# Moving nine adds of squares from VectorE to GpSimd, and a scaled copy ahead of a square, in a two-layer decoder step

## The chip, the core and the metric

The kernel runs on one core of a Trainium2 chip, in one launch. The metric is the device time of that launch in microseconds. Engines are named as in the profile: PE is TensorE, PEld its weight loads, DVE is VectorE, ACT is ScalarE, POOL is GpSimd and SP is SyncE, which issues most of the transfers.

## What is computed

One inference step of a two-layer decoder for 512 prompt tokens and 8 sample tokens (520 together), width 1024, all in 32-bit floats. Each layer is a half-weighted SwiGLU block, a token mixer, and a second SwiGLU block; the first layer mixes by causal window means, the second by window attention. A norm stands ahead of every one of them, and one at the end:

```
def _rmsnorm(x, g):
    xf = x.astype(jnp.float32)
    y = xf * lax.rsqrt(jnp.mean(xf * xf, axis=-1, keepdims=True) + EPS)
    return (y * g.astype(jnp.float32)).astype(x.dtype)

def _swiglu(x, wg, wu, wd):
    return (jax.nn.silu(x @ wg) * (x @ wu)) @ wd

# every layer l:
x = x + 0.5 * _swiglu(_rmsnorm(x, norm_g[l, 0]), ...)
h = _rmsnorm(x, norm_g[l, 1])
x = x + mixer(h)
x = x + 0.5 * _swiglu(_rmsnorm(x, norm_g[l, 2]), ...)
# at the end
y = _rmsnorm(x, final_norm_g)
```

The outputs are y of both groups, the last rows of the pooling input, and the windows of keys and values. The change touches only the sums of squares that the norms need.

## The kernel before

The residual stream lies transposed in SBUF: eight channel tiles x of 128 channels by 520 tokens. Weights stream from HBM as raw tiles; each is split into a rounded high part and a remainder (`wh` by ACT, `wl` by DVE, both 128x512), and every product is three matmuls: high by high, high by low, low by high. Activations are split likewise (`xh` and `xl`, `th` and `tl`, `hh` and `hl`). Part of the products are done by a seven-product scheme, which needs sums of weight blocks: S, summed by transfers on POOL's queue (L649, L372), and sums on DVE (L379, L386).

A norm is not applied ahead of a product. The products take x scaled by g alone, and the token's factor is put in behind them. So a norm runs beside the products: ACT squares each x tile into `sq` (two buffers), DVE adds the eight squares into `acc` (a copy for the first tile, seven adds), PE sums `acc` over the channels by matmuls with a vector of ones (L845, "column sums"), DVE works out the root in a chain of small instructions that ends in `r_tok` (L857 to L869), and PE turns `r_tok` round into a row for all partitions (L885, L886), which ACT copies into `R`.

Three places of this kind concern the change:

- *Behind the first half layer*, ahead of the pooling mixer, the function `delayed` squares tile k when it is finished (L1482) and adds the square when the next tile comes (L1459, L1461). The last tile's work is pinned to the written order. PE passes from the down projection to the mixer's first products (L1700) and then to the column sums.
- *At the start of the second half layer* (the first layer's second SwiGLU block), eight calls of `square` (L816, L818, L823) stand ahead of it.
- *In the tail*, `final_after` calls `square` and then `scaled` for each finished x tile; `scaled` (L2444) makes the copy `xg`, scaled by the final norm's g, that PE turns back into token rows (`turn`, L2424 and L2425).

What sets the order. In the first place and the tail, the tile framework's scheduler, but for what is pinned. In the second, a planner written in the kernel, the class `Queues`: every step is added with an engine ("A" for ACT, "V" for DVE, "P" for PE, "N" for others), a cost, a due time and the keys that it reads and writes; PE's products advance the planner's clock, and a step is issued into its engine's order when its predecessors are done by the planner's account. A step on "N" costs nothing there:

```
cost = 0 if eng == "N" else cols * self.unit if eng == "P" else 50 + 0.93 * cols if eng == "A" else 70 + 1.04 * cols
```

The engines then run their orders one after the other, with waits on one another where data need it.

Of the kernel before, what the change touches and what calls it, by code (L numbers as in the profile page):

```python
# [15 lines left out]
ALU = mybir.AluOpType  # L16
# [4 lines left out]
KT = 8  # L21
# [3 lines left out]
TOK = SP + NS  # L25
# [522 lines left out]
def yoco_step(ctx, tc, ins, outs):  # L548
    nc = tc.nc
# [3 lines left out]
    V, S, T = nc.vector, nc.scalar, nc.tensor  # L553
# [16 lines left out]
    Q = Queues(1344)  # L570
# [3 lines left out]
    def duo():  # L574

        cnt[0] += 1
        k = Q.key("ps", 4)
        Q.bank = (*k, 0), (*k, 1)
        return pools[0].tile([P, 2, 512], F32, tag="ps", name=f"ps{cnt[0]}")
# [9 lines left out]
    def pair(tags, shape, dtype=F32R):  # L589

        return tuple(big.tile(shape, dtype, tag=t, name=t) for t in tags)
# [6 lines left out]
    def by_slots(on, busy=0):  # L598

        W.pin = lambda ins: ins  # L600
        if on:
            pinned.enter_context(
                tc.manual_schedule(
                    engines={mybir.EngineType.PE, mybir.EngineType.DVE, mybir.EngineType.Activation}
                )
            )
            W.begin_slots(Q)
            Q.start(W.ng, busy)
            W.plan()
        else:  # L610
            Q.stop()
            W.q = None
            assert W.ns == W.nh and not Q.pending
            pinned.close()

    def seq(ins):

        return later(ins) if ordered[0] else ins
# [17 lines left out]
    def later(ins):  # L636

        return tc.keep_in_program_order(ins)


    W = Weights(nc, rawp, splp, 2, 5)
# [131 lines left out]
    acc = cp.tile([P, TW], F32, name="acc")  # L773
# [4 lines left out]
    def gcol(n, k):  # L778
        return gT[:, n * 8 + k : n * 8 + k + 1]
# [29 lines left out]

        return bank[:, :H].rearrange("p (a b) -> p b a", b=2)  # L810

    def square(k, pool, tag, order=lambda ins: ins):
        sq = pool.tile([P, TOK], F32, tag=tag, name="sq", bufs=1 if tag == "rp0" else 2)
        key = Q.key(tag, 2)
        G = (*key, 0), (*key, 1)
        Q.add("A", 520, lambda: order(S.activation(sq, x[k], AF.Square)), W.ng + 2, (), G)  # L816
        if k == 0:
            Q.add("V", 520, lambda: order(V.tensor_copy(acc[:, :TOK], sq)), W.ng + 2, G, (("acc",),))  # L818
        else:
            Q.add(  # L820
                "V",
                520,
                lambda: order(V.tensor_tensor(acc[:, :TOK], acc[:, :TOK], sq, op=ALU.add)),  # L823
                W.ng + 2,
                G,
                (("acc",),),
            )

    pss_ = [None]
    nu = [2]  # L830

# [606 lines left out]
    def ff_pool():  # L1438
        return tc.tile_pool(name="ff", bufs=2, reuse_waits="tile")

    def deferred(n, tmp, tag, tags, lst, w=TOK):

        def f(k):
            z = pair(tags, [P, w])
            split(tuple(a[:, :TOK] for a in z), x[k], gcol(n, k))
            lst.append(z)
            square(k, tmp, tag)

        return f

    def delayed(n, tmp, tag, tags, lst, w):

        made = {}

        def rest(k):
            z, sq = made.pop(k)
            pin = later if k + 1 >= PIN0 else seq
            if k == 0:
                pin(V.tensor_copy(acc[:, :TOK], sq))  # L1459
            else:  # L1460
                pin(V.tensor_tensor(acc[:, :TOK], acc[:, :TOK], sq, op=ALU.add))  # L1461
            if k < KT - 2:
                low(k, z, pin)
            else:
                lows.append((k, z))

        def low(k, z, pin):
            h, l = (a[:, :TOK] for a in z)
            pin(V.scalar_tensor_tensor(l, x[k], gcol(n, k), h.bitcast(F32), op0=ALU.mult, op1=ALU.subtract))

        lows = []

        def f(k):
            if k:
                rest(k - 1)
            z = pair(tags, [P, w])
            sq = tmp.tile([P, TOK], F32, tag=tag, name="sq")
            high = lambda: S.activation(z[0][:, :TOK], x[k], AF.Copy, scale=gcol(n, k))
            if k < KT - 1:
                high()  # L1480
            pin = later if k + 1 >= PIN0 else seq
            pin(S.activation(sq, x[k], AF.Square))  # L1482
            if k == KT - 1:
                high()
            lst.append(z)
            made[k] = z, sq
            if k == KT - 1:
                rest(k)
                for v in lows:
                    low(*v, later)  # L1490

        return f

    def start_hooks(tmp, n, tt, late, norm_tok=rstd_tok):

        steps = sums(tmp, n, tt, W.next_sum())
        step = lambda: next(steps, None)
        there[0] = False
        none = lambda: None

        norm0 = norm_tok

        def norm_all():
            rstd_all()
            known()

        kinds = {"-": none, "s": step, "n": norm0, "a": norm_all}

        def many(word):
            def f():  # L1510
                for c in word:
                    kinds[c]()

            return f

        return [many(w) for w in late.split()]
# [3 lines left out]
    with ff_pool() as tmp:  # L1520
# [69 lines left out]
        first = duo(), duo()  # L1590
# [13 lines left out]
        for k in range(KT):  # L1604
            if k > 1:
                quarter(k, 0)
            if k + 2 < KT:
                x_tile(k + 2)()
            quarter(k, 1)
            if k == 1:  # L1610
                ws += [W.get(), W.get()]
            if k > 2:
                W._split(k + 1)
            for i in {}.get(k, ()):
                square(i, tmp, "g", later)
        by_slots(True, 0)
        for k in range(0, KT):
            square(k, tmp, "g")
# [52 lines left out]
    with tc.tile_pool(name="pm", bufs=2, reuse_waits="tile") as pm:  # L1671
# [33 lines left out]
        def high(gi, tau):  # L1705
            r = r_tok[:, tau : tau + 1] if tau < 4 else r5
            later(S.activation(back(zs[gi][tau][0]), apart(places[gi][tau]), AF.Copy, scale=r))
# [103 lines left out]
    with ff_pool() as tmp:  # L1811


        later(nc.sync.dma_start(pool_sample[0, :, 0:14, :], state_pool[0, :, 1:15, :]))
        for dst, src in ((k_win_s, cache_k), (v_win_s, cache_v)):
            later(
                nc.sync.dma_start(
                    dst[:, 0:127].rearrange("b s g d -> b s (g d)"), src[:, 1:128].rearrange("b s g d -> b s (g d)")
                )
            )  # L1820
        later(nc.sync.dma_start(sraw, attn_sinks.broadcast_to([P, 16])))
        for b in range(NS):
            later(nc.sync.dma_start(sink_s[b * 16 : (b + 1) * 16, 0:1], attn_sinks.rearrange("l h -> h l")))
        by_slots(True, 2)
        for m in range(KT):
            square(m, tmp, "g")
        tt = {}
        ffn(1, tmp, mov2, start_hooks(tmp, 2, tt, "- - ns s a s s s s s s"), tt, HH, deferred(N_KV, tmp, "g", XX, movk))

# [153 lines left out]
    with tc.tile_pool(name="at", bufs=2, reuse_waits="tile") as at:  # L1983
# [61 lines left out]
        class Unit:  # L2045
# [71 lines left out]
            def turn(self, bi):  # L2117
                if bi == 0:
                    self.pts = {}
                    self.both = {}  # L2120
                b = self.bs[bi]
                self.both[bi] = single()
                for kt in (0,) if b == 0 else (0, 1):
                    for e in range(2):
                        z = self.sm[:, 2 * bi + e, 256 - self.keys(bi) + kt * P :][:, :P]
                        later(T.transpose(self.both[bi][:, kt * 256 + e * P : kt * 256 + (e + 1) * P], z, ident))  # L2126
# [48 lines left out]
        first = W.ng  # L2175
# [223 lines left out]
    with ff_pool() as tmp:  # L2399
# [41 lines left out]
        def scaled(k, c):  # L2441
            if k not in xgs:
                xgs[k] = tmp.tile([P, TOK], F32, tag=("t", "sa")[k % 2], name="xg")
            seq(S.activation(xgs[k][:, c], x[k][:, c], AF.Copy, scale=gcol(N_FIN, k)))  # L2444

        def final_after(k):
            square(k, tmp, "g")
            scaled(k, slice(0, TOK))
            if k == 1:
                later(S.activation(warm, ones[:, 0:1], AF.Sqrt))  # L2450
            waiting.append(k)
            W.ahead += 2
            if len(waiting) > 2:
                k = waiting.pop(0)
                turn(k)(*engines[k % 2])
# [45 lines left out]
        def tail(hs):  # L2501
# [118 lines left out]
            ordered[0] = False  # L2620

        ffn(3, tmp, mov6, start_hooks(tmp, 5, tt, "ss ns sss a ss s", norm_tok), tt, HH, final_after, by_parts=tail)


# [29 lines left out]
```

## Time and profile before

| What | Value |
|---|---|
| Time, median of 3 runs | 1519.8 us (1519.19 to 1526.01) |
| Profiled execution, its own time | 1520.76 us |
| Its span, first to last instruction | 1517.8 us |
| Mean granted PE clock | 0.998 |
| PE busy | 1503.1 us (99%) |
| DVE busy | 1385.1 us (91%) |
| ACT busy | 991.1 us (65%) |
| POOL busy | 308.0 us (20%) |

Times in the profile are in microseconds from the first instruction of that execution. A matmul's end is modelled, and matmuls overlap; a busy PE need not be one at its peak. Idle time of an engine stands in brackets in front of the instruction that ended it, with what released it. L and a number is a line of the kernel before.

### The profile page before, as it was taken

The numbers are of one execution on the slowest core, as the hardware profiler recorded it, in microseconds if no ns is written. First come the engines' busy times: TensorE is split into PE (matmuls) and PEld (weight loads), VectorE is DVE, ScalarE is ACT, GpSimd is POOL, SyncE is SP. The second block draws the span as 40 slices with busy tenths as digits, with TensorE's granted clock in tenths as the row PEclk, the third lists the DMA queues.
The fourth block names the chain that finished last, engine by engine and source line by source line (L and its number), as shares of the span: only waits on it lengthen the run. The fifth ranks groups of instructions, "written<-read, shape, count | busy, mean of one in ns | idle before, by whom it ended". The sixth has DMA issues, their size and how long they took to land.

```text
span 1517.8 us, 34874 instructions
## 1 busy us (share of the span) xinstructions
PE 1503.1 (99%) x13342; PEld 1489.3 (98%) x13342; DVE 1385.1 (91%) x2790; ACT 991.1 (65%) x2025; POOL 308.0 (20%) x346
## 2 busy tenths in 40 slices
PE   9999999999999999999999999999999999999997
PEld 8999999999999999999999999999999999999997
DVE  6999999979999999879999999876887899999977
ACT  6765665657675675656665675655886666666655
POOL 1122222000122222100322222101551122222200
PEclk9999999999999999999999999999999999999999
DMA  9589899763599999835898998854313589999941
GB/s 246 121 194 208 182 202 207 178 182 100 118 205 199 194 204 199 177 119 127 198 204 189 197 206 194 184 175 115 75 43 92 111 185 198 200 194 193 207 132 57
DMA packets 418834, 254.61 MB, mean 168 GB/s; under 512 B 13134, under 2 KB 399174, under 8 KB 418628
## 3 DMA queue, kind: packets, MB, share of 16 engines
q1 hardware_dynamic: 339822, 187.60, 44.7%
q0 software_dynamic: 75520, 60.00, 28.4%
q10 hardware_dynamic: 3326, 4.79, 1.0%
q8 instruction: 104, 1.70, 0.5%
q14 instruction: 62, 0.51, 0.1%
HBM read 218.07 MB, written 6.11 MB: 148 GB/s over the span
## 4 chain that ended last, share of the span: by engine, by line
PE 85%; DVE 8%; ACT 3%; DMA 2%; issue 1%; POOL 0%; DVEq 0%; ACTq 0%
PE ps L935 61%; PE ps L905 17%; DVE wl L476 2%; DMA pr<-in_bands_dram 1%; PE pv L2153 1%; ACT wh L472 1%; PE ps L2068 1%; PE pv L2126 1%; PE pv L1700 1%; PE pv L1749 1%; DMA S<-in_ffn_w_down_dram 0%; DVE acc L823 0%; PE ps L2521 0%; PE ps L2530 0%; PE pv L905 0%
## 5 line engine op out<-in xcount | busy, mean ns | idle before, releaser
L472 ACT ACTIVATE wh<-raw 128x512 fp32r<-128x512 f32 (+1 forms) x725 | 443.8, 624 | 181.1 <-PE ps L935 69.0
L476 DVE TENSOR_TENSOR wl<-raw,wh 128x512 fp32r<-128x512 f32 (+1 forms) x725 | 482.8, 681 | 21.1 <-ACT wh L472 19.5
L935 PE MATMUL ps<-th,wh 128*128 128x260 f32 x1216 | 334.5, 275 | 0.3 <-DVE sb L1241 0.3
L935 PE MATMUL ps<-tl,wh 128*128 128x260 f32 x1216 | 334.4, 275 | 0.0
L935 PE MATMUL ps<-th,wl 128*128 128x260 f32 x1216 | 334.4, 275 | 0.0
L935 PE MATMUL ps<-xh,wh 128*128 128x260 f32 x896 | 247.2, 276 | 0.3 <-ACT sb L1209 0.3
L935 PE MATMUL ps<-xl,wh 128*128 128x260 f32 x896 | 246.4, 275 | 0.0
L935 PE MATMUL ps<-xh,wl 128*128 128x260 f32 x896 | 246.4, 275 | 0.0
L935 PEld LDWEIGHTS ps<-th,wh 128*128 128x128 f32 x1216 | 231.0, 190 | 0.5 <-DVE sb L1241 0.5
L935 PEld LDWEIGHTS ps<-tl,wh 128*128 128x128 f32 x1216 | 231.0, 190 | 0.0
L935 PEld LDWEIGHTS ps<-th,wl 128*128 128x128 f32 x1216 | 231.0, 190 | 0.0
L935 PE MATMUL ps<-hh,wh 128*128 128x260 f32 x656 | 181.0, 276 | 0.1
L935 PE MATMUL ps<-hl,wh 128*128 128x260 f32 x656 | 180.6, 275 | 0.4 <-DVE hl L624 0.3
L935 PE MATMUL ps<-hh,wl 128*128 128x260 f32 x656 | 180.4, 275 | 0.0
L649 POOL DMA_DIRECT2D S<-in_ffn_w_up_dram x76 | 100.3, 1327 | 373.6 <-DMA S<-in_ffn_w_up_dram 122.3
L935 PEld LDWEIGHTS ps<-xh,wh 128*128 128x128 f32 x896 | 170.2, 190 | 1.5 <-ACT sb L1209 0.8
L935 PEld LDWEIGHTS ps<-xh,wl 128*128 128x128 f32 x896 | 170.2, 190 | 0.0
L935 PEld LDWEIGHTS ps<-xl,wh 128*128 128x128 f32 x896 | 170.2, 190 | 0.0
L372 POOL DMA_DIRECT2D raw<-raw x108 | 95.0, 880 | 358.4 <-DMA raw<-in_ffn_w_up_dram 58.8
L935 PEld LDWEIGHTS ps<-hh,wh 128*128 128x128 f32 x656 | 124.6, 190 | 1.2 <-ACT ps L1280 1.2
L935 PEld LDWEIGHTS ps<-hl,wh 128*128 128x128 f32 x656 | 124.6, 190 | 0.8 <-DVE hl L624 0.8
L935 PEld LDWEIGHTS ps<-hh,wl 128*128 128x128 f32 x656 | 124.6, 190 | 0.0
(382 smaller groups left out, 3653.0 us busy)
## 6 DMA issues: line engine op xcount, KB each, us to landing
raw<-in_ffn_w_gate_dram SPq DMA_DIRECT2D x87, 512.0 KB, 4.8
raw<-in_ffn_w_up_dram SPq DMA_DIRECT2D x87, 512.0 KB, 7.1
raw<-in_ffn_w_down_dram SPq DMA_DIRECT2D x128, 256.0 KB, 5.1
raw<-raw POOLq DMA_DIRECT2D x108, 256.0 KB, 4.6
S<-in_ffn_w_up_dram SPq DMA_DIRECT2D x76, 256.0 KB, 4.5
S<-in_ffn_w_up_dram POOLq DMA_DIRECT2D x76, 256.0 KB, 5.6
raw<-in_ffn_w_down_dram SPq DMA_DIRECT2D x16, 768.0 KB, 4.4
S<-in_ffn_w_down_dram SPq DMA_DIRECT2D x32, 256.0 KB, 3.0
```

The costliest lines, as they stand in the source:

```text
L372: G.dma_start(blk(raw, 2, 1), blk(raw, 1, 1), accum_op=ALU.add)
L472: self.pin(self.nc.scalar.activation(views[0], src, AF.Copy))
L476: self.pin(self.nc.vector.tensor_tensor(l, src, h.bitcast(F32), op=ALU.subtract))
L649: return [ld(lambda t: t, a), lambda t: nc.gpsimd.dma_start(t, b, accum_op=ALU.add)]
L905: ins = T.matmul(banks[:, hf, :H], a[:, kk, :], two(hcols(b, hf)), start=(first and i == 0), stop=(last and i == 2),)
L935: T.matmul(bank[:, :H], a[:, kk, :], two(b), start=(not more and kk == 0 and i == 0), stop=(kk == 3 and i == 2), skip_group_check=more,)
L1700: later(T.matmul(o, a[:, c], two(b[:, kk, :]), start=(n == 0), stop=(n == 5)))
L1749: later(T.matmul(o, zz[tau][z][:, c], two(b), start=(i == 0), stop=(i == len(lst) - 1)))
L2068: later(T.matmul(o, q_[rows, qc], k_[rows, kc_], start=(i == 0), stop=(i == 2)))
L2126: later(T.transpose(self.both[bi][:, kt * 256 + e * P : kt * 256 + (e + 1) * P], z, ident))
L2153: later(T.matmul(o, a, two(p_[:, kc_]), start=(n == 0), stop=(n == 3 * len(kts) - 1)))
```

## The change

In `delayed`, the first square's copy into `acc` is left out, and the squares of the tiles 0 to 5 are added on POOL: tile 1's to tile 0's, then one after the other, five adds. The squares of tiles 6 and 7 are still added on DVE. In `square`, an argument `others` does the same for the first tiles; only the second half layer's call gives it, with 3, so two adds go to POOL. In `final_after`, the scaled copy is written ahead of the square.

```diff
@@ def square
-    def square(k, pool, tag, order=lambda ins: ins):
+    def square(k, pool, tag, order=lambda ins: ins, others=0):
         sq = pool.tile([P, TOK], F32, tag=tag, name="sq", bufs=1 if tag == "rp0" else 2)
         key = Q.key(tag, 2)
         G = (*key, 0), (*key, 1)
         Q.add("A", 520, lambda: order(S.activation(sq, x[k], AF.Square)), W.ng + 2, (), G)
-        if k == 0:
+        if k < others:
+            if k == 0:
+                begun.append(sq)
+                Gs.append(G)
+                return
+            first = begun.pop() if k == 1 else acc[:, :TOK]
+            Q.add(
+                "N",
+                0,
+                lambda: nc.gpsimd.tensor_tensor(acc[:, :TOK], first, sq, op=ALU.add),
+                W.ng + 2,
+                (*G, *(Gs.pop() if k == 1 else ())),
+                (("acc",),),
+            )
+        elif k == 0:
             Q.add("V", 520, lambda: order(V.tensor_copy(acc[:, :TOK], sq)), W.ng + 2, G, (("acc",),))
         else:
@@ def delayed, rest(k)
             if k == 0:
-                pin(V.tensor_copy(acc[:, :TOK], sq))
+                made["sq"] = sq
+            elif k < KT - 2:
+                nc.gpsimd.tensor_tensor(acc[:, :TOK], made.pop("sq") if k == 1 else acc[:, :TOK], sq, op=ALU.add)
             else:
                 pin(V.tensor_tensor(acc[:, :TOK], acc[:, :TOK], sq, op=ALU.add))
@@ second half layer
         for m in range(KT):
-            square(m, tmp, "g")
+            square(m, tmp, "g", others=3)
@@ def final_after
         def final_after(k):
+            scaled(k, slice(0, TOK))
             square(k, tmp, "g")
-            scaled(k, slice(0, TOK))
```

How this moves instructions. From the function `square` on, the changed kernel's lines are numbered 14 to 17 higher; a number behind x, ps or raw is a buffer's, and x_81 to x_88 are the eight channel tiles.

POOL, from the last weight sum of the first half layer to the first of the second (S and raw are weight sums, hrow the rows of the pooling output), before:

```order
L372 DMA raw_4181<-raw_4181 128x512
L1783 DMA out_dram<-hrow 15x512
L1784 DMA out_dram<-hrow 8x512
L1783 DMA out_dram<-hrow 15x512
L1784 DMA out_dram<-hrow 8x512
L649 DMA S<-in_ffn_w_up_dram 128x4x128
```

and now:

```order
L372 DMA raw_4181<-raw_4181 128x512
L1476 TENSOR_TENSOR acc<-sq 128x520
L1476 TENSOR_TENSOR acc<-acc,sq 128x520 x4
L1800 DMA out_dram<-hrow 15x512
L1801 DMA out_dram<-hrow 8x512
L1800 DMA out_dram<-hrow 15x512
L1801 DMA out_dram<-hrow 8x512
L826 TENSOR_TENSOR acc<-sq 128x520
L826 TENSOR_TENSOR acc<-acc,sq 128x520
L649 DMA S<-in_ffn_w_up_dram 128x4x128
```

Five adds come in behind the first half layer, and two stand between the output transfers and the first weight sum S.

PE, in the first plain tile of the second half layer (ps_5603 and ps_5604 are its two banks before, ps_5602 and ps_5603 now; four times three rows are one weight tile), before, with the column sums behind the fourth weight tile and ahead of the next tile:

```order
L905 MATMUL ps_5604<-xh,wh 128x260 x2
L905 MATMUL ps_5604<-xl,wh 128x260 x2
L905 MATMUL ps_5604<-xh,wl 128x260 x2
L845 MATMUL ps_5695<-ones,acc 128x1 x5
L905 MATMUL ps_5751<-xh,wh 128x260 x2
```

and now:

```order
L920 MATMUL ps_5602<-xh,wh 128x260 x2
L920 MATMUL ps_5602<-xl,wh 128x260 x2
L920 MATMUL ps_5602<-xh,wl 128x260 x2
L860 MATMUL ps_5704<-ones,acc 128x1 x5
L920 MATMUL ps_5603<-xh,wh 128x260 x2
```

The column sums now stand behind the third weight tile of that plain tile, 12 rows earlier; the turn of r_tok (L885) keeps its place. On ACT one weight half instead of three now stands ahead of the third square there, and on DVE one split (`wl`) stands between the adds and three behind the last one, instead of five behind it.

ACT, in the tail, where xg is the scaled copy, before:

```order
L816 ACTIVATE sq<-x_81 128x520
L2444 ACTIVATE xg<-x_81,gT 128x520
L816 ACTIVATE sq<-x_82 128x520
L2444 ACTIVATE xg<-x_82,gT 128x520
L2450 ACT_TABLE_LOAD
```

and now:

```order
L2461 ACTIVATE xg<-x_81,gT 128x520
L816 ACTIVATE sq<-x_81 128x520
L2461 ACTIVATE xg<-x_82,gT 128x520
L816 ACTIVATE sq<-x_82 128x520
L2467 ACT_TABLE_LOAD
```

Each pair of square and scaled copy is the other way round, for all five tiles that pass here.

More of the change, by code (lines that the diff above doesn't have):

```diff
@@ L827, in square @@
             )
+    begun, Gs = [], []
     pss_ = [None]
```

## The prediction

> **What bounds the kernel now.** I read the page first, then PE's waits, then the timelines of the three places that the diff touches. Rows of engines give busy us, share and instructions.
>
> ```profile
> span 1517.8 us, 34874 instructions
> PE 1503.1 (99%) x13342; PEld 1489.3 (98%) x13342; DVE 1385.1 (91%) x2790; ACT 991.1 (65%) x2025; POOL 308.0 (20%) x346
> PEclk9999999999999999999999999999999999999999
> ```
>
> TensorE (PE) sets the time: busy for 1503.1 of 1517.8, at the full granted clock. No matmul is added or removed, so the change can only win PE's idle time, 14.7 us in all, part of it before the first matmul and after the last. Of PE's waits (total us, times, longest) four lie at or behind what changes:
>
> ```profile
> PE ps L885 <- DVE r_tok L869: 1.1, 1, 1.1
> PE pv L845 <- DVE acc L1461: 1.1, 1, 1.1
> PE ps L2424 <- ACT xg L2444: 0.4, 1, 0.4
> PE ps L935 <- ACT sb L1209: 0.3, 1, 0.3
> ```
>
> Together 2.9 us, 0.2% of the span. VectorE (DVE) at 91% is not the bound; its load counts only where one of these four waits ends on it.
>
> **Place 1, end of the first half layer.** Rows are start, duration, engine, line, operation, tiles, in brackets the idle time before. The last two are groups of one tile's instructions, durations as min/median/max in ns.
>
> ```profile
> 338.96 0.39 PE L905 MATMUL ps<-hh,wl 128*128 128x260 f32 x2
> 343.76 0.28 PE L1700 MATMUL pv<-th,xl 128*128 128x256 f32 x1
> 345.14 1.27 PE L845 MATMUL pv<-ones,acc 128*128 128x1 f32 x10 [1.11 <-DVE acc L1461]
> 342.20 0.69 DVE L1401 TENSOR_TENSOR u<-ps,R 128x520 f32<-128x520 f32 x1
> 344.38 0.70 DVE L1461 TENSOR_TENSOR acc<-acc,sq 128x520 f32<-128x520 f32 x1 [0.15 <-ACT sq L1482]
> 325.97 0.62 ACT L1482 ACTIVATE sq<-x 128x520 f32<-128x520 f32 x1
> 340.17 0.62 ACT L1482 ACTIVATE sq<-x 128x520 f32<-128x520 f32 x1
> L1461 DVE TENSOR_TENSOR acc<-acc,sq x7: 692/696/702, 327.1 to 344.4; 128x520 f32<-128x520 f32 x7
> L1459 DVE COPY acc<-sq x1: 423/423/423, 324.8 to 324.8; 128x520 f32<-128x520 f32 x1
> ```
>
> PE ends the last tile at 339.35, but DVE takes that tile up only at 342.20: it is 2.85 us behind. The final add ends at 345.08, and PE's column sums (L845) start at 345.14. Matmuls follow each other every 0.11 there, so PE was ready at 343.87 and loses 1.27.
>
> Removed from DVE: the copy (0.42) and five adds (0.70 each), 3.9 us by their durations, about 3.4 since neighbours overlap by 0.08. That is more than the 2.85 of backlog. DVE then takes the last tile at 339.4, and the rest is a chain: u 0.6, x 0.7, the square 0.7, the add 0.7: 342.1. PE is ready at 343.87, so the 1.27 is won, with 1.8 to spare, unless GpSimd (POOL) is late.
>
> What one POOL add costs is the unknown: the trace has no two-input operation on POOL. The nearest rows (mean ns after the comma), and two stretches in which DVE works beside POOL:
>
> ```profile
> L2115 POOL TENSOR_SCALAR sm<-sm,den 128x256 f32<-128x256 f32 x33 | 34.2, 1046 | 15.0 <-DVE den L2108 13.9 <-PE ps L905 0.9
> L2115 POOL TENSOR_SCALAR sm<-sm,den 128x128 f32<-128x128 f32 x6 | 3.9, 661 | 5.1 <-DVE den L2108 5.1
> 1086.25 2.63 POOL L2115 TENSOR_SCALAR sm<-sm,den 128x256 f32<-128x256 f32 x2
> 1085.99 1.28 DVE L476 TENSOR_TENSOR wl<-raw,wh 128x512 fp32r<-128x512 f32 x2
> 1129.60 0.93 POOL L2115 TENSOR_SCALAR sm<-sm,den 128x256 f32<-128x256 f32 x1 [0.87 <-PE ps L905]
> 1129.99 0.68 DVE L2038 TENSOR_TENSOR xl<-qraw,xh 128x512 fp32r<-128x512 f32 x1
> ```
>
> From 128 to 256 elements 385 ns are added, 3.0 ns an element; 520 elements then take 1046 + 264 x 3.0 = 1.84 us. Lower bound: DVE's own 0.70. Upper bound, if two inputs are read one after the other: 0.28 fixed + 520 x 6.0 = 3.4. I take 1.8, nearest to the one-input rows. The Trainium skill ("GPSIMD Engine Reference", section "Performance versus the Vector engine") measured 4497 ns for a two-input add of 2048 elements, by proportion an estimate of 1.14 for 520; the sum below would be 0.7 us lower by it.
>
> The stretch at 1086 shows a second cost: two POOL operations take 2.63 where one alone takes 0.93, and the excess of 0.8 compares with the 1.0 that DVE's two-input pair, ending at 1087.27, still ran on when the first began. So an add that is issued into such work starts late, by 0.6 to 1.2. The stretch at 1129 shows that DVE is not slowed in turn: an operation that began inside the POOL one took its usual 0.68.
>
> The five adds run from 326.6 (second square done). The fifth's square, done at 340.8 now, comes about 2.2 earlier, since DVE skips four adds and waits a little more for ACT: 338.6. At 1.8 that add ends at 340.4, before DVE wants the sum. The margin is gone if 326.6 + five adds + 1.5 for the two adds left on DVE passes 343.9, so above 3.2 us an add. POOL's queue is empty here. A square waits for the add two before it (two buffers); behind it on ACT stand the next tile's scaled copies and weight halves, which at 1.8 an add and squares 2.5 to 3.5 apart do not wait.
>
> **Place 2, start of the next half layer.**
>
> ```profile
> 376.15 0.39 PE L905 MATMUL ps<-xh,wh 128*128 128x260 f32 x2
> 378.83 1.25 PE L845 MATMUL ps<-ones,acc 128*128 128x1 f32 x10
> 379.93 0.47 PE L905 MATMUL ps<-xh,wh 128*128 128x260 f32 x2
> 384.00 0.65 PE L885 MATMUL ps<-ident,r_tok 128*128 128x128 f32 x4 [1.14 <-DVE r_tok L869]
> 374.11 0.68 DVE L1855 COPY sinks<-sraw 128x8 f32<-128x8 f32 x8
> 374.77 0.69 DVE L823 TENSOR_TENSOR acc<-acc,sq 128x520 f32<-128x520 f32 x1
> 375.56 3.12 DVE L823 TENSOR_TENSOR acc<-acc,sq 128x520 f32<-128x520 f32 x4
> 378.60 3.09 DVE L476 TENSOR_TENSOR wl<-raw,wh 128x512 fp32r<-128x512 f32 x5
> 381.95 0.16 DVE L857 TENSOR_SCALAR nv<-ps 128x5 f32<-128x5 f32 x1
> 370.80 1.66 ACT L472 ACTIVATE wh<-raw 128x512 fp32r<-128x512 f32 x3
> 372.36 1.15 ACT L816 ACTIVATE sq<-x 128x520 f32<-128x520 f32 x2
> 368.17 1.38 POOL L649 DMA_DIRECT2D S<-in_ffn_w_up_dram  x1
> 379.64 0.90 POOL L372 DMA_DIRECT2D raw<-raw  x1 [10.09 <-DMA S<-in_ffn_w_up_dram]
> 400.83 0.62 ACT L472 ACTIVATE wh<-S 128x512 fp32r<-128x512 f32 x1
> ```
>
> Now: the last add ends at 378.68, and PE comes to its column sums at 378.83, just in time. In the new order these stand one weight tile, 2.68 us (376.15 to 378.83), earlier: the planner gives POOL's adds no time. With the 1.27 from place 1, PE gets there at 374.88. When is the sum ready? ACT's third square started at 372.36; with 1.27 off and two weight halves fewer ahead (1.04 of 1.66) it starts at 370.05 and is done at 370.6. POOL's first add starts when the four output DMAs are issued (368.17 less 1.27 = 366.9), and ends at 368.7, in time for that square's buffer. The second ends at 370.6 + 1.8 = 372.4. Behind it on DVE come five adds (0.61 apart), one weight split (0.6), the small copies (0.7) and some 0.3 for the last square: 4.7, since the fifth square also waits for POOL. The sum is ready at 377.2 and PE loses 2.3, a **new wait**.
>
> After it PE spends 1.10 on the sums (378.83 to 379.93) and now two weight tiles of 2.75 before L885: 377.2 + 1.1 + 5.5 = 383.8, against 384.00 before. DVE reaches r_tok after three splits (1.8), a difference (0.35) and its chain of 2.05 (381.95 to 384.00): 381.4, so the old wait of 1.14 (1.30 with the ramp) is gone. In balance: -1.27 + 2.3 - 1.30 = about **-0.2 us**. If the second add is held up by 0.6, it is +0.4; at 3.4 us an add, +3.0; at 0.7, about -1.3.
>
> POOL's weight-sum DMA (L649) moves behind two adds, from 368.17 to about 372.4, and would land some 5 to 7 later. The one that waits next for POOL's queue is L372 at 379.64, and the sum S is first read at 400.83: up to 20 us cover it. Without that cover its delay would be paid in full, some 4 us.
>
> **Place 3, the tail.**
>
> ```profile
> 1483.39 0.64 ACT L816 ACTIVATE sq<-x 128x520 f32<-128x520 f32 x1 [0.61 <-DVE x L1402]
> 1483.94 0.71 ACT L2444 ACTIVATE xg<-x,gT 128x520 f32<-128x520 f32 x1
> 1483.90 0.39 PE L905 MATMUL ps<-hh,wl 128*128 128x260 f32 x2
> 1484.70 0.66 PE L2424 MATMUL ps<-ident,xg 128*128 128x128 f32 x4 [0.41 <-ACT xg L2444]
> ```
>
> The scaled copy goes first: it starts at 1483.39 instead of 1483.94 and ends at 1484.10. PE, ready at 1484.12, no longer waits: **-0.5 us**. The square is 0.6 later, and DVE's add of it with it; its reader, the column sums some 16 us later, has that cover. Without it, the 0.6 would come back.
>
> The wait of 0.3 at L935 and some like it follow in the reordered stretch up to about 480 us; new order may remove or add such, ±0.5, taken as -0.3.
>
> **Sum**: -0.2 - 0.5 - 0.3 = -1.0 us. The profiled execution took 1520.76 us (its span and 2.96 around it), so 1519.8 by it; the median of the runs shown, 1519.8, lies 1.0 lower. Against the median I predict 1518.8 us. 0.5% is 7.6 us, about what a measurement of this kernel can tell from no change: all of this is below it.
>
> **Rivals.**
> (a) *The sums are not waited for in place 2.* Then -1.27 - 1.30 - 0.5 - 0.3 = -3.4: 1516.4. It needs the last add done by 374.9, so the second POOL add by 370.1, before its own square is done (370.6). For it speaks only that my replay of ACT's order may be off. 8%.
> (b) *Slow adds on POOL*: at 3.4 us each the five end at 343.6, and the wait of place 1 stays; in place 2 the second add ends at 375.7, the sum is ready at 380.4, L885 comes at 387.0: +3.0 - 0.5, 1522.3. It decides from 3.2 us an add. For it: two inputs, and adds held up by DVE's two-input work; against it the linear estimate. 14%.
> (c) *POOL holds DVE up*: if each add stops DVE's two-input instructions while it reads, 1.8 less the fixed 0.3, the five cost DVE 7.5 less 0.7 of waits that it has anyway. Place 1 ends at 342.1 + 6.8 = 348.9, PE loses 5.0 instead of 1.27; with place 2 at a loss of 2.3 to 4.3 the total is +4.3 to +6.3, about 1525: slower than before. It decides from 0.35 us of hold an add (1.8 of margin over five). Against it the row at 1129.99, though with a shorter POOL operation. 15%. The Trainium skill ("SBUF — State Buffer", section "Who interferes with whom") states this rule: a two-input DVE instruction and a GpSimd instruction that reads SBUF block each other, whoever is first. The rows bear out the half in which POOL waits, not the other.
> (d) That the change does not do what it says is ruled out by the order of the instructions.
>
> **How the numbers follow.** The forecast has 60%, (a) 8, (b) 14, (c) 15, anything else 3. The forecast's own range is 1517 to 1520.5 (adds of 0.7 to 2.5, small waits ±0.5, run to run 0.5). 1516.4 to 1523.2 takes in (a), (b) and the lower edge of (c). Faster by over 0.5% would need 7.6 us of the 14.7: 2%. Slower by as much needs (c) at its worst, or adds above 5 us: 4%. The rest, 94%, is within.
>
> **What would show it.** Right: L845 in place 1 without a wait on acc; a new wait of about 2 us on acc at the next L845; none at L885, none at the first L2424; POOL's adds near 1.8 us, longer where they start inside DVE's splits. Wrong: adds over 3.2 us; DVE splits or x updates of over 1 us beside a POOL add; or a new wait above 0.5 us behind 384 us.

## The result and the profile after

The changed kernel took 1525.76 us (median of 22 runs, 1523.07 to 1531.45), the kernel before beside it 1521.65 us (22 runs, 1519.01 to 1526.01). The ratio is 1.0026 with a 95% interval of 1.0018 to 1.0034: 4.0 us slower, between 2.7 and 5.2. That is inside the 0.5% which counted as no change, but the sign is clear, and the time lies above the predicted range. The median of before came out 1.9 higher here than in the three runs from which the prediction started; against it, -1.0 was forecast.

The profiled execution of the changed kernel, from its page and from the list of PE's waits:

```profile
span 1523.9 us, 34888 instructions
PE 1506.3 (99%) x13342; PEld 1493.4 (98%) x13342; DVE 1386.8 (91%) x2781; ACT 991.0 (65%) x2025; POOL 317.7 (21%) x353
```

```profile
PE ps L860 <- DVE acc L837: 3.6, 2, 2.8
PE pv L860 <- DVE acc L1478: 1.8, 1, 1.8
PE pv L1717 <- DVE u L1416: 0.8, 1, 0.8
```

Two things stand in the first rows. DVE has nine instructions fewer (2781 for 2790: seven adds moved to POOL, two copies fell away) and is busy *longer* (1386.8 for 1385.1). And PE, which has the same matmuls, is busy 3.2 longer, besides waiting more. Of the waits, the one at r_tok (1.14) and the one at the tail's xg (0.41) are gone; the one in the first place grew from 1.11 to 1.78, one of 0.80 stands ahead of it, and one of 2.75 is new in the second place. (L860 is L845 of before, moved down by the added lines; L1717 is L1700, L1478 is L1461.)

**First place.** Timelines of PE, POOL and DVE in the changed kernel:

```profile
342.02 0.38 PE L1717 MATMUL pv<-th,xh 128*128 128x256 f32 x1 [0.80 <-DVE u L1416]
348.76 1.31 PE L860 MATMUL pv<-ones,acc 128*128 128x1 f32 x10 [1.78 <-DVE acc L1478]
328.48 1.35 POOL L1476 TENSOR_TENSOR acc<-sq 128x520 f32<-128x520 f32 x1 [41.84 <-ACT sq L1499]
331.76 1.30 POOL L1476 TENSOR_TENSOR acc<-acc,sq 128x520 f32<-128x520 f32 x1 [1.93 <-ACT sq L1499]
336.21 1.30 POOL L1476 TENSOR_TENSOR acc<-acc,sq 128x520 f32<-128x520 f32 x1 [3.15 <-ACT xh L630]
340.04 1.29 POOL L1476 TENSOR_TENSOR acc<-acc,sq 128x520 f32<-128x520 f32 x1 [2.54 <-ACT xh L630]
344.13 1.73 POOL L1476 TENSOR_TENSOR acc<-acc,sq 128x520 f32<-128x520 f32 x1 [2.80 <-ACT xh L630]
328.58 1.80 DVE L1417 SCALAR_TENSOR_TENSOR x<-u,x 128x520 f32<-128x520 f32 x1
332.27 1.35 DVE L1486 SCALAR_TENSOR_TENSOR xl<-x,gT,xh 128x520 fp32r<-128x520 f32 x1
336.86 0.67 DVE L631 TENSOR_TENSOR xl<-sts,xh 128x8 fp32r<-128x8 f32 x1
340.08 1.28 DVE L631 TENSOR_TENSOR xl<-sts,xh 128x8 fp32r<-128x8 f32 x1
344.63 1.26 DVE L631 TENSOR_TENSOR xl<-sts,xh 128x8 fp32r<-128x8 f32 x1
348.00 0.70 DVE L1478 TENSOR_TENSOR acc<-acc,sq 128x520 f32<-128x520 f32 x1 [0.15 <-ACT sq L1499]
```

The same kinds of DVE rows before, with POOL idle:

```profile
327.81 0.70 DVE L1402 SCALAR_TENSOR_TENSOR x<-u,x 128x520 f32<-128x520 f32 x1
330.76 0.76 DVE L1469 SCALAR_TENSOR_TENSOR xl<-x,gT,xh 128x520 fp32r<-128x520 f32 x1
342.12 0.16 DVE L631 TENSOR_TENSOR xl<-sts,xh 128x8 fp32r<-128x8 f32 x1
```

Read the five POOL rows and the five DVE rows beside each other. Each POOL add has one DVE instruction with it that is far longer than its kind: x<-u,x 1.80 where it takes 0.69 elsewhere in this stretch, xl<-x 1.35 for 0.76, and the small 128x8 difference 0.67, 1.28 and 1.26 for 0.16. And each of the five ends a fixed time behind POOL, short for a small instruction and longer for a wide one: the add of 340.04 ends at 341.33 and the small difference at 341.36; the add of 331.76 ends at 333.06, the wide difference at 333.62, 0.56 later. DVE's instruction did not run slowly, it stood until POOL was done. The five excesses are 1.11, 0.59, 0.51, 1.12 and 1.10: 4.4 us, more than the 3.4 that the change took from DVE. The last add is done at 348.70.

**Second place.** Timelines of PE, POOL, DVE and ACT in the changed kernel:

```profile
383.74 2.03 PE L860 MATMUL ps<-ones,acc 128*128 128x1 f32 x10 [2.75 <-DVE acc L837]
372.77 1.30 POOL L826 TENSOR_TENSOR acc<-sq 128x520 f32<-128x520 f32 x1
376.70 1.64 POOL L826 TENSOR_TENSOR acc<-acc,sq 128x520 f32<-128x520 f32 x1 [2.63 <-ACT sq L816]
377.11 1.79 DVE L1750 SCALAR_TENSOR_TENSOR xl<-x,gT,xh 128x520 fp32r<-128x520 f32 x1
382.09 1.51 DVE L837 TENSOR_TENSOR acc<-acc,sq 128x520 f32<-128x520 f32 x2
378.38 0.64 ACT L816 ACTIVATE sq<-x 128x520 f32<-128x520 f32 x1 [1.23 <-POOL acc L826]
```

The pattern repeats: the second add holds one DVE instruction (1.79 for 0.75), ACT's fourth square waits 1.23 for its buffer, and the sum is ready at 383.60. PE wanted it at 380.99.

**The clock.** Behind the long waits PE is slower. Columns are the stretch, its length, busy time and instructions of PE, PEld, DVE, ACT and POOL, then the granted clock, the DMA share and GB/s:

```profile
350.00:353.30 3.30, 3.30 (x17) 3.30 (x17) 2.67 (x14) 2.07 (x7) 0.00 (x0) 0.50 0.77 320
353.30:357.00 3.70, 3.70 (x35) 3.70 (x35) 3.40 (x9) 3.46 (x9) 0.00 (x0) 1.00 0.03 1
384.00:387.40 3.40, 3.40 (x17) 3.40 (x18) 3.13 (x11) 1.40 (x3) 2.07 (x2) 0.50 0.98 137
387.40:390.80 3.40, 3.40 (x18) 3.40 (x18) 2.19 (x8) 0.00 (x0) 0.00 (x0) 0.50 1.06 290
```

The clock is halved for one stretch of 3.4 us behind the wait of 1.78, and for two behind the wait of 2.75. The same stretches before:

```profile
350.00:353.30 3.30, 3.30 (x32) 3.30 (x32) 3.08 (x8) 3.06 (x9) 0.00 (x0) 1.00 0.03 1
387.40:390.80 3.40, 3.40 (x33) 3.40 (x32) 3.29 (x8) 2.72 (x7) 0.87 (x1) 1.00 0.66 103
```

PE does 17 or 18 matmuls where it did 32 or 33, so each stretch costs about 1.7 us.

**Where the 6.1 us between the two profiled spans lie**, following the same matmul through both: +1.9 by 39 us (a half-clock stretch that the change is nowhere near), +3.3 in the first place (0.80 + 0.67 of waits, 1.7 of clock), -0.6 on the way, +4.9 in the second (2.75 - 1.14 of waits, 3.4 of clock), -1.8 up to 476 us by small waits that went, and -1.7 near 1106 us, where before had such a stretch and the changed kernel none. The first and the last are no work of the change and nearly cancel.

The other executions can be asked through their mean granted clock. It is 0.9942 over the 22 runs of the changed kernel and 0.9971 over the 103 runs of the kernel before that the experiments below have beside them. Over 1521 us that is 4.4 us a run, known to about 0.6 and as much as the whole 4.0: what the change gains and loses in waits nearly cancels, and half clock makes the difference. One run of an experiment below, with one-input operations, took 1711 us at a granted clock of 0.851 and is left out of its ratio.

**Tail.**

```profile
1489.71 0.73 ACT L2461 ACTIVATE xg<-x,gT 128x520 f32<-128x520 f32 x1 [0.61 <-DVE x L1417]
1490.50 0.65 PE L2441 MATMUL ps<-ident,xg 128*128 128x128 f32 x4
```

The copy runs first, and PE's transposition follows its last product without a wait.

### The profile page after: what moved, and what is told of

It is laid out like the page before. It is cut to its first block, busy times and chain, and to the rows that moved or that the text cites. A ratio compares the mean times of both kernels' runs of the same rounds, so it can differ in the third digit from the quotient of the medians.

```text
span 1523.9 us, 34888 instructions
## 1 busy us (share of the span) xinstructions
PE 1506.3 (99%) x13342; PEld 1493.4 (98%) x13342; DVE 1386.8 (91%) x2781; ACT 991.0 (65%) x2025; POOL 317.7 (21%) x353
## 4 chain that ended last, share of the span: by engine, by line
PE 91%; DVE 5%; ACT 2%; DMA 2%; issue 1%; POOL 0%; SPq 0%; DVEq 0%; ACTq 0%
PE ps L950 66%; PE ps L920 18%; PE pv L2170 1%; DMA pr<-in_bands_dram 1%; PE pv L2143 1%; PE ps L2085 1%; PE pv L1766 1%; PE pv L1717 1%; PE ps L860 0%; DVE wl L476 0%; DVE acc L837 0%; PE ps L2538 0%; PE ps L2547 0%; DMA raw<-in_ffn_w_gate_dram 0%; PE pv L920 0%
```

## Experiments

The theory, T: while POOL reads two inputs, DVE's instructions with two inputs in SBUF stand still, so DVE's backlog grows where it was to shrink; PE's longer waits then bring stretches of half clock. Against it stood that the order in the second place is to blame, that POOL's adds are late by themselves, and that the clock is mere chance. Each kernel below was timed in five rounds beside the kernel before.

### Each of the three edits alone

The first edit alone (the lines of `delayed`), the second alone (`others=3`), the third alone (the two lines of `final_after`), each as in the diff above.

> Only the first edit: GpSimd makes five adds and the copy falls away behind the first half layer; everything behind and the tail as before. Theory T (a GpSimd add holds DVE's two-input instructions, 0.5 to 1.1 us each; PE's longer waits bring stretches of 3.4 us at half the granted clock, 1.7 us each): the last add on DVE ends later than PE wants it, PE waits 1.5 to 2 us at the column sums (1.11 before) and about 0.8 at an earlier matmul, a half-clock stretch follows, in all +1.5 to +4 us. Rival R1 (the order in the second place alone made the changed kernel slow): this kernel gains 1.3. Rival R2 (the GpSimd adds are themselves too late): the wait is there, but DVE's instructions keep their usual lengths (0.69, 0.76, 0.16) and DVE itself waits for GpSimd's sum.

> Only the second edit: GpSimd makes two adds at the start of the second half layer, the column sums stand one weight tile earlier on PE; the first place and the tail as before. Theory T: PE waits 2 to 3 us for the sum at these column sums, the 1.14 at the wait for r_tok is gone, and behind the long wait the clock is halved for 3.4 or 6.8 us: +1 -1.2 +1.7 to 3.4, in all +2.5 to +4.5 us against before. Rival R1' (the wait alone, clock not affected): +1 to +1.5. Rival (a) of the prediction, no wait: -1.3.

> Only the third edit: in the tail the scaled copy goes ahead of the square, all else as before. By the prediction's step and by every theory held now: no wait of PE on xg at the first L2424 (0.41 before), time 0.5 us lower than before. If the edit costs something later (the square, and with it DVE's add, 0.6 later), a new wait appears at the last column sums and the gain is gone.

Ratios to before: first edit 1.0015 (1.0005 to 1.0025), +2.3 us; second 1.0012 (1.0003 to 1.0021), +1.8; third 1.0005 (0.9994 to 1.0017), not told from zero. The sum, +4.1 without the third, agrees with the +4.0 of the whole change; each of the two is known to about 1.5 us.

With the first edit alone PE waits 0.83 and 1.78, and the same DVE rows are held; half clock follows for 3.4 us. With the second alone it waits 2.74, with 3.4 us of half clock behind it, and the wait for r_tok is gone. So both places lose by themselves; the order in the second is not the cause of the first. In the tail the trace shows the 0.41 gone: the same matmul stands 2.79 behind before's ahead of the transposition and 2.27 behind it. The timing can't show these 0.5 us: its interval is 3.5 us wide, and this profile had two half-clock stretches more than that of before (behind a wait of 1.23 in the first place, and near 1110 us).

### The adds kept, but on 8 columns

```
-nc.gpsimd.tensor_tensor(acc[:, :TOK], ..., sq, op=ALU.add)
+nc.gpsimd.tensor_tensor(acc[:, :8], ...[:, :8], sq[:, :8], op=ALU.add)
```

> As the kernel with only the first edit, but each of the five GpSimd adds works on 8 of the 520 columns; the rest of the additions of the first six tiles is left out, so DVE is relieved in the same way and GpSimd works a fraction of the time. Theory T: DVE's instructions keep their lengths, the last add is ready before PE asks for it, the wait at the column sums (1.11 before) is gone, no half-clock stretch: 1.3 us below before, as the prediction had it for the first place. Rival R2 (order or issue of the instructions, not the time that GpSimd reads, makes DVE late): the wait stays above 1 us.

> As the kernel with only the second edit, but its two GpSimd adds work on 8 of the 520 columns; the rest of the additions of the first three tiles is left out. PE still comes to the column sums one weight tile earlier. If the wait of 2.74 there comes from what GpSimd's adds last and hold (theory T): two adds of 1.3 to 1.6 less and a hold of 1.1 less bring the sum some 1 to 2.5 us earlier, and a wait of 0.3 to 1.7 stays. If it comes from the earlier place in the order and DVE's own queue alone: the wait stays at 2.5 or more.

These kernels leave out the rest of those additions, so they show times and nothing else. In the first place this is the decisive run. POOL, DVE and PE:

```profile
335.71 0.20 POOL L1461 TENSOR_TENSOR acc<-acc,sq 128x8 f32<-128x8 f32 x1 [3.12 <-ACT xh L630]
335.75 0.18 DVE L631 TENSOR_TENSOR xl<-sts,xh 128x8 fp32r<-128x8 f32 x1
341.49 0.70 DVE L1463 TENSOR_TENSOR acc<-acc,sq 128x520 f32<-128x520 f32 x1 [0.16 <-ACT sq L1484]
343.34 0.62 PE L845 MATMUL pv<-ones,acc 128*128 128x1 f32 x5
```

The instructions and their order on DVE are those of the first edit; only the time that POOL works on each add is gone. No DVE row is held, the last add ends at 342.19, and the column sums follow the products without a wait. The prediction's chain gave 342.1; this execution runs 0.5 ahead of that of before, so 342.7 on before's clock. PE asks for the sum at 343.34, 1.15 later. The time is 0.9984 of before (0.9975 to 0.9992), -2.4 us. The full width of POOL's adds, with the clock that follows, thus costs 4.7 us in the first place, against the same edit with full adds.

In the second place the wait falls from 2.74 to 1.57 and the time to 0.9995 (0.9984 to 1.0007). So 1.2 of that wait is what POOL's adds last and hold, and 1.6 comes from the order and DVE's own queue. T expected 0.3 to 1.7 to stay. Half clock followed this shorter wait too.

### The column sums at their old place

In the kernel with the second edit alone, the planner is given a price for the two adds:

```
-cost = 0 if eng == "N" else ...
+cost = cols if eng == "N" else ...
 Q.add("N",
-      0,
+      1500,
       lambda: nc.gpsimd.tensor_tensor(acc[:, :TOK], first, sq, op=ALU.add), ...
```

> As the kernel with only the second edit, but the planner reckons 1500 ns for each of the two GpSimd adds where it reckoned none; by this PE's column sums go back to their old place, one weight tile later, and PE's whole order is that of the kernel before. Theory T: the wait of 2.74 at the column sums falls by the 2.7 of a weight tile to under 0.5; the wait for r_tok (1.14 before) comes back, at 1 to 1.5; no half-clock stretch of its own; time within 1 us of before. If the adds and their hold matter beyond the order, 1 us or more of wait at the column sums stays and the time is 1 to 2 us above before.

```profile
382.36 0.24 PE L860 MATMUL ps<-ones,acc 128*128 128x1 f32 x1 [2.18 <-DVE acc L837]
373.73 3.56 POOL L826 TENSOR_TENSOR acc<-acc,sq 128x520 f32<-128x520 f32 x1 [3.18 <-ACT sq L816]
374.26 1.88 DVE L476 TENSOR_TENSOR wl<-raw,wh 128x512 fp32r<-128x512 f32 x3
377.32 0.64 ACT L816 ACTIVATE sq<-x 128x520 f32<-128x520 f32 x1 [2.63 <-POOL acc L826]
```

The wait did not fall under 0.5: it is 2.18, a weight tile later. The planner also put three weight splits ahead of the adds on DVE, and now it is POOL that stands: its second add takes 3.56, from 373.73 to 377.29, and gets on only when DVE's run of two-input instructions ends at 376.14. The lock works both ways. Which engine gets on when both want to is not told by who came first: three splits that start at 374.26 go ahead of an add that stands since 373.73, whereas in the first place DVE's next instruction stood behind the add. The wait for r_tok did not come back, no half clock followed, and the time was 1.0005 of before (0.9996 to 1.0013). My expectation for this run failed. The run can't say what the place of the column sums alone is worth, because the price moved DVE's order with it.

### POOL's reading beside an untouched DVE

Nothing is taken from DVE; POOL gets five operations of its own behind DVE's adds.

```
+if 0 < k < KT - 2:
+    nc.gpsimd.tensor_tensor(sq, x[k], x[k], op=ALU.add)          # two inputs
+    nc.gpsimd.tensor_scalar(sq, x[k], 1.0, None, op0=ALU.mult)   # or: one input
+    nc.gpsimd.memset(sq, 0.0)                                    # or: none
```

> Nothing is taken from DVE: the kernel before, with five GpSimd operations added behind the first half layer, each a two-input add of 128x520 from a tile of the activations into a square's tile that is no longer needed, issued when DVE's own add of that square is done. The orders of PE, DVE and ACT stay as they were. Theory T (what GpSimd reads for 1.3 us holds DVE's instructions with two inputs in the on-chip memory): five holds of 0.5 to 1.1 us stand in DVE's rows; DVE's backlog at the last tile grows from 2.85 to about 7, PE waits some 3 to 5 us in all instead of 1.11, and the time is 3 to 7 us over before with the half-clock stretches behind. Rival R2 (no hold; DVE was late in the changed kernel for another reason): DVE's rows keep 0.69, 0.76 and 0.16, the waits stay, time as before.

> As the run before in this call, but the five GpSimd operations only write (a fill with zeros of the same 128x520 tile, no input). Theory T, in its narrow form that it is GpSimd's reading that holds DVE: no DVE row is longer than before, PE waits about 1.1 at the column sums, time as before within 1 us. In its wide form, any GpSimd access to the on-chip memory: holds as long as the fill lasts, and the time rises with them.

> As the earlier run with five GpSimd adds beside an unchanged DVE, but the five GpSimd operations read one input (a multiplication by 1.0 of 128x520 into the same unneeded tile). The row on which the prediction relied, at 1129.99, stood beside a one-input GpSimd operation. If a one-input operation does not hold DVE: DVE rows keep their lengths, PE waits about 1.1 to 1.3 at the column sums, time as before within 1 us. If it holds DVE as the two-input adds did: rows longer by 0.2 to 0.9, waits of PE of 3 in all, time about 3 above before, and the row at 1129.99 was no evidence either way.

Two inputs, POOL and DVE:

```profile
332.60 1.52 POOL L1463 TENSOR_TENSOR sq<-x 128x520 f32<-128x520 f32 x1 [1.78 <-DVE xl L631]
343.10 1.50 POOL L1463 TENSOR_TENSOR sq<-x 128x520 f32<-128x520 f32 x1 [1.24 <-DVE acc L1461]
333.13 1.41 DVE L447 TENSOR_TENSOR wl<-raw,wh 128x384 fp32r<-128x384 f32 x1
343.62 1.01 DVE L631 TENSOR_TENSOR xl<-sts,xh 128x8 fp32r<-128x8 f32 x1
```

None, that is a fill:

```profile
328.10 0.53 POOL L1463 MEMSET sq<- 128x520 f32 x1 [41.97 <-DVE acc L1461]
328.04 0.69 DVE L1402 SCALAR_TENSOR_TENSOR x<-u,x 128x520 f32<-128x520 f32 x1
```

One input:

```profile
332.29 2.44 POOL L1463 TENSOR_SCALAR sq<-x 128x520 f32<-128x520 f32 x1 [1.06 <-DVE xl L631]
341.69 1.96 POOL L1463 TENSOR_SCALAR sq<-x 128x520 f32<-128x520 f32 x1 [0.74 <-DVE acc L1461]
327.99 3.24 POOL L1463 TENSOR_SCALAR sq<-x 128x520 f32<-128x520 f32 x1 [41.84 <-DVE xl L631]
332.81 0.55 DVE L447 TENSOR_TENSOR wl<-raw,wh 128x384 fp32r<-128x384 f32 x1
333.88 0.55 DVE L447 TENSOR_TENSOR wl<-raw,wh 128x384 fp32r<-128x384 f32 x1
342.20 0.58 DVE L631 TENSOR_TENSOR xl<-sts,xh 128x8 fp32r<-128x8 f32 x1
```

With two inputs DVE is held by 0.87 (1.41 for 0.54) and 0.85 (1.01 for 0.16), and by 0.1 to 0.3 three times; PE's waits grow to 0.81 and 2.27, and the time is 1.0020 of before (1.0011 to 1.0030), +3.1 us: the low end of what T gave, since POOL's first add stood itself (2.79 instead of about 1.5) and in three of the five cases DVE came to u<-ps, which reads PSUM, in that time. A fill holds nothing: DVE's x<-u,x beside it took 0.69, PE waited 1.19, the ratio is 0.9998 (0.9987 to 1.0009). With one input the two still meet, but it costs DVE little: three of POOL's operations take 1.96, two stretch to 2.44 and 3.24 while DVE's splits keep their usual 0.55, and just one DVE row is held, by 0.4. It gets on at 342.78, 0.87 ahead of the end of POOL's operation, and in the last 0.8 of the others DVE's two-input rows keep their lengths (0.55 at 333.88, with POOL busy until 334.73). A two-input add held DVE until its end. PE waited 1.65; the ratio is 0.9999 (0.9990 to 1.0008). So the harm does not hang on POOL being busy: 2.3 of holds in sum for five two-input adds, 0.4 for five longer one-input operations, none for a fill. Whether the number of inputs decides that, or how long an operation reads, these runs don't separate; in two of the five one-input cases DVE also happened to be at u<-ps.

### Idle time and the clock, without POOL

Ahead of the last add in the first place, one or two more DVE adds into a tile that is no longer needed:

```
+if k == KT - 1:
+    for _ in range(1):   # or range(2)
+        pin(V.tensor_tensor(made['old'], x[k], x[k], op=ALU.add))
```

> No GpSimd work: the kernel before, with one more two-input add of 128x520 on DVE (into a tile that is no longer needed) ahead of the last add of the squares in the first place, so that PE waits one add longer: 1.11 + 0.70 = 1.8, as long as in the changed kernel. If the longer idle time itself brings a stretch of 3.4 us at half clock: that stretch stands right behind it, and the time is 0.7 to 2.4 us above before. If half clock there needs GpSimd or is chance: no such stretch behind it, time 0.7 above before.

> As the run before, with two more adds on DVE: PE's wait is 1.11 + 1.40 = 2.5, near the 2.75 of the changed kernel's second place. If idle time brings half clock: a stretch of 3.4 or 6.8 us behind it, 1.4 + 1.7 to 3.4 above before, less what before itself pays for such stretches in some of its runs. If not: 1.4 above before.

One add more, the stretches around the column sums:

```profile
343.50:346.90 3.40, 1.68 (x16) 1.49 (x14) 3.37 (x7) 2.47 (x7) 0.00 (x0) 1.00 0.67 287
346.90:350.30 3.40, 3.40 (x17) 3.40 (x17) 2.76 (x14) 2.20 (x8) 0.00 (x0) 0.50 0.44 177
```

PE waits 1.72, and half clock follows, with POOL doing nothing. The time is 1.0013 of before (1.0002 to 1.0023), +2.0 for 0.6 of added wait. With two adds PE waits 1.92 (not 2.5: PE itself came 2.9 later, 1.7 of it by a half-clock stretch at 37 us, and DVE's chain only 2.45), one stretch follows, and the ratio is 1.0015 (1.0006 to 1.0023). Not every time, though: over the fourteen profiles of this case, of the ten waits of 1.57 to 2.75 in these two places nine were followed by half clock, and of the sixteen of 1.06 to 1.37 three, all three at the column sums of the first place (of six there) and none at r_tok (of ten). The second add here shows no dose beyond the first.

The traces say more about when. In each profile with several half-clock stretches, these start whole multiples of 3.413 us apart (in the changed kernel at 35.85, 349.87 and 384.01, that is 92 and 10 steps), so they follow a fixed grid whose place differs from execution to execution. Add up the columns that PE's matmuls stream in each 3.413 us of that grid, with their widths in the traces: between 20 and 1000 us, in all fourteen profiles, half clock follows each of the 18 steps with at most 3130 columns and none of those with 3330 or more; a usual step has 7800. That fits both findings: a wait counts most ahead of column sums, which stream one column each, and the wait of 2.18 above, which was not followed, lay across two steps. Near 1105 us, among the small products of the attention, the count does not divide the steps so cleanly.

### A version that gives POOL nothing

```
+sq = tmp.tile(...) if k else acc[:, :TOK]      # delayed: ACT writes the first square into the sum
-if k == 0:
-    pin(V.tensor_copy(acc[:, :TOK], sq))
-if k < KT - 2:
+if k < KT - 3:                                 # the sixth tile's low half behind the last add
     low(k, z, pin)
 ...                                            # final_after as in the change
```

> A version meant to beat both kernels, with no work on GpSimd: ACT writes the first square straight into the sum (DVE's copy of 0.42 falls away), the low halves of the sixth tile are computed behind the last add (0.75 and 0.16 off the chain ahead of it), and the tail's scaled copies go ahead of the squares. By the chain in DVE's rows the last add ends 1.0 to 1.2 earlier, PE's wait of 1.11 falls to under 0.2, and the wait at the first L2424 (0.41) is gone: 1.5 us below before. If only the clock's stretches decide what is measured at this size, no difference shows.

```profile
344.37 0.70 DVE L1459 TENSOR_TENSOR acc<-acc,sq 128x520 f32<-128x520 f32 x1 [0.16 <-ACT sq L1480]
345.13 0.38 PE L845 MATMUL pv<-ones,acc 128*128 128x1 f32 x2
```

PE starts the column sums at 345.13 after 0.11 of idle, and the first L2424 without a wait. The last add ends at 345.07, the same moment as before; but in this execution PE came to the end of the tile 1.0 later, by a half-clock stretch at 35 us, so against PE the add is 1.0 earlier. (The second edit's profile has such a stretch too, with the first place as before: there the add came 1.2 later with PE, and the wait stayed at 1.06.) A new wait of 0.71 came 13 us later, at the mixer's second products, for DVE's hl, and one of 1.37 stands at r_tok (1.14 before). The ratio is 0.9985 (0.9977 to 0.9994): 2.3 us faster than before, where 1.5 was expected. By these ratios it beats both kernels, though it was not timed beside the changed one. Its mean granted clock is 0.9975 over the 11 runs, for 0.9972 beside it: half clock makes 0.4 of the 2.3, known to about 0.6, and the rest is the waits.

## Why the prediction was wrong

Point by point, by its own steps.

- **The hold of DVE: the step that failed.** "The stretch at 1129 shows that DVE is not slowed in turn" rested on one row, a DVE instruction of the usual 0.68 inside a POOL operation of 0.93. That POOL operation had *one* input. The run with one-input operations shows that those held DVE once in five, and let it on 0.87 ahead of their end; the two-input adds held DVE by 0.5 to 1.1 each, 0.89 on average, where 0.35 was named as the point from which rival (c) decides. The prediction named its rows one-input when it priced an add; in weighing the hold it noted only that the operation was shorter.
- **Rival (c)** gave about 1525, at 15%; 1525.76 came. Its mechanism is right, and the Trainium skill's rule ("SBUF — State Buffer", section "Who interferes with whom") that goes with it, weighed and put aside, holds in both halves for two-input adds: DVE held 1.1 us by POOL, POOL held to 3.56 by DVE. That whoever is first goes on was not borne out where POOL stood and three more splits went ahead. The rival's sizes are a different mix: not 7.5 of hold but 4.4, and most of the loss is the clock, which it did not have. So that its 1525 was hit is in part luck.
- **The chain of the first place** was right but for 0.6: 342.1 for the last add without holds, 342.19 measured with the short adds in an execution that ran 0.5 ahead. The margin was 1.15 instead of 1.8, and holds of 4.4 took it.
- **POOL's price** was mis-sized: 1.8 taken, 1.29 to 1.35 measured where POOL was not held itself. The Trainium skill's estimate of 1.14 was nearer. It did not matter, since an add that lasts 1.3 still holds what waits for it.
- **The second place.** A new wait of 2.3 was forecast, 2.75 came (2.74 with this edit alone); the wait at r_tok went, as said. The hold of 1.0 on xl and the square that waits for POOL are in this 2.75; the shorter adds made up for most of it, so that the size came out so near is luck.
- **What follows a wait** is the second step that failed. It was not in the sum at all: each wait was priced at its own length, the forecast's own new wait of 2.3 too. Two stretches of half clock in the second place and one in the first added some 5 us to the profiled execution, more than all changed waits, and the mean granted clock of the single runs says 4.4.
- **The tail** was right, -0.5, by the trace; too small to be timed.
- **The small waits** up to 480 us: -0.3 taken, -1.8 measured.

## What to carry to other kernels

Before work goes from VectorE to GpSimd, count inputs: here a two-input GpSimd operation beside a VectorE busy with two-input work in SBUF gained nothing, since one of them stood while the other read; it passed only VectorE's instructions that read PSUM. A row that clears a suspect must be of the same kind as what is added: same number of inputs, same memory. And where PE is always busy, price a wait of 1.5 us and more with the half clock behind it, a shorter one too where it stands ahead of matmuls of few columns, and look for work that can move behind the awaited instruction on its own engine before looking for another engine.

## What the runs showed of the hardware

- Between two-input adds of POOL and DVE's instructions with two inputs in SBUF the exclusion is whole, and a tiny instruction pays like a large one: a 128x8 difference of 0.16 took 1.28.
- One-input POOL operations of 1.96 held DVE by 0.4 in sum, two-input adds of the same size by 2.3. Whether the number of inputs or the time that is spent reading decides that is open.
- PE's half clock comes in stretches of 3.4 us or twice that, at 1.7 us each, on a grid of 3.413 us that is fixed within an execution. Waits of 0.80 and 1.06 us were enough for one in some profiles, both ahead of column sums. The Trainium skill ("TensorE: Matmul & The Clock Gate", section "Part 1: The HAM clock gate (the "warmup" mystery)") describes a free-running window of 3413 ns, whose place varies from run to run. The traces agree in the length and in the grid; an idle time as long as the window was not needed in any run here, the longest such wait was 2.75.
- At 33 us PE waits 0.80 in every one of the fourteen profiles, and half clock follows in five of them. Single executions of the kernel before lie 6 us apart in one comparison (1517.88 to 1524.10) and 10 in another (1518.05 to 1528.15), so an edit worth 0.5 us is seen in the trace alone.
